# A Strassen decoder trunk: the first quarter of a round and late plain weights without adding DMAs, and a store moved to GpSimd

## The chip, the cores and the metric

The kernel runs on one core of one Trainium2 chip. The metric is the device time of one execution in microseconds. A profiled execution gives the trace: which instruction ran when on TensorE (PE for matmuls, PEld for weight loads), VectorE (DVE), ScalarE (ACT), GpSimd (POOL) and SyncE (SP), when each DMA was issued and landed, and what ended each wait.

## The reference, cut to what matters

Two layers over 512 tokens of width 1024, all in float32. The part that the change touches most is the squared-ReLU MLP of each layer, `h = relu(rms_norm(x) @ w1)`, `x = x + (h * h) @ w2`, with a hidden width of 4096:

```
def sq_relu_mlp(xn, w1, w2):
    h = jax.nn.relu(xn @ w1)
    return (h * h) @ w2

for i in range(2):
    x = x + (diff_attention if i == 0 else retention)(rms_norm(x, norm_mix[i]), ...)
    x = x + sq_relu_mlp(rms_norm(x, norm_mlp[i]), mlp_w1[i], mlp_w2[i])
    gate = jax.nn.sigmoid(rms_norm(x, norm_pe[i]) @ pe_w_gate[i])
    x = x + gate * (p[i] @ pe_w_up[i])
```

The product `p[i] @ pe_w_up[i]` is called the embedding here; layer 1's is the second one.

## The kernel before

**Every float32 product is three matmuls.** A matrix is split into a high part (`hi`, the value rounded to the type float32r) and a low part (`lo`, what is left), and `mm3` (L264 to L266) issues high x high, high x low and low x high. So each weight block that comes from HBM, 128x1024 floats or 512 KB, needs a high and a low tile before TensorE can use it. The tiles are called `wh` and `wl`; there are five buffers of each, and three of the raw block (`raw`).

**How a weight is made (class Weights).** `order` lists all blocks and mixed kinds, 280, in the order of use. `W.next()` hands out the next pair and makes blocks up to four ahead. A plain block is loaded by SP (L91 or L100), ScalarE copies it to `wh`, and then one of two things happens. Where `by_dma` is false, VectorE subtracts: `lo = raw - hi` (L105). Where it is true, ScalarE writes `-raw` to `lo` (L93) and GpSimd issues a DMA that adds `raw` onto `lo` (L94); the raw buffer is read by that DMA until it lands. `by_dma` is set after the first value projection and cleared in the MLP of layer 0.

**The MLP.** Each layer's MLP runs in four chunks of 1024 hidden columns. A chunk first makes eight hidden tiles (`ph`, L768 and after): 24 matmuls of 512 columns each, then ReLU, scale, square, and the split. In the first three chunks the second product goes by Strassen's method (Winograd's form) in two rounds, r = 0 and r = 1, through `mix_round`. A round takes seven products ("kinds") in the order of `MIX`: a11, s1, s2, s4, s3, a12, a22. Each has two halves of 12 matmuls of 256 columns, and its result is added to `x` by VectorE (L729) before the bank is used again. The banks are called `py{layer}{chunk}{round}{bank}`; a11, s2, s3 and a22 use bank b. TensorE takes r = 0 in a slightly mixed order, r = 1 in strict order, a11 first.

**How a kind's weights are made (`mixed`, L108 to L155).** The kinds are quarters of `w2` or sums of them: a11, a21, a22 and a12 are fetched by SP (L118), s1 = a21 + a22 (L129), s2 = s1 - a11 (L132), s4 = a12 - s2 (L136) and s3 = a11 - a21 (L139) on VectorE. ScalarE copies the quarter or sum to `wh` (L146). For a11 and a22 ScalarE also writes `lo = -hi` (L149), and a DMA issued by GpSimd adds the quarter onto it from HBM (L150), a second read of that quarter. For the other five kinds VectorE subtracts (L154). Because of the look-ahead of four, the last quarters of a round and the first kinds of the next are made one behind the other while the round's middle products run.

**What sets the order.** The tile framework orders each engine's instructions by a planner from the program's order and its own estimates; each engine then takes its queue strictly in that order. SP's loads keep the program's order. So an instruction that waits holds back all behind it on its engine.

**The second embedding.** After the retention stage, TensorE makes eight tiles `pu` (L1028), ScalarE copies each out of its bank (L1030), and a DMA issued by ScalarE writes it to DRAM (L1031), from where the last stage reads it. On GpSimd, the last gate products (L1009) come before that point, and the running sum of squares of the next norm (L314) after it.

Of the kernel before, what the change touches and what calls it, by code (L numbers as in the profile page):

```python
# [13 lines left out]
ALU = mybir.AluOpType  # L14
# [50 lines left out]
class Weights:  # L65
# [42 lines left out]
    def mixed(self, kind, w, first):  # L108

        nc, mix = self.nc, self.mix  # L110
        i = len(self.made)

        def source(b):
            return w[first + b // 2 : first + b // 2 + 3 : 2, :, b % 2 * T : b % 2 * T + T].rearrange("j p n -> p j n")

        def fetch(b):
            raw = self.pool.tile([P, 1024], F32, name=f"raw{i}_{b}", tag="raw", bufs=RAW_BUFS)
            self.tc.keep_in_program_order(nc.sync.dma_start(out=raw.rearrange("p (j n) -> p j n", j=2), in_=source(b)))  # L118
            return raw

        def fresh():
            return self.sums.tile([P, 1024], F32, name=f"mix{i}", tag="mix", bufs=2)

        if kind == "a11":
            t = mix["a11"] = fetch(0)
        elif kind == "s1":
            mix["a21"], a22 = fetch(2), fetch(3)
            t = mix["s1"] = fresh()
            nc.vector.tensor_tensor(out=t, in0=mix["a21"], in1=a22, op=ALU.add)  # L129
        elif kind == "s2":  # L130
            t = mix["s2"] = fresh()
            nc.vector.tensor_tensor(out=t, in0=mix["s1"], in1=mix["a11"], op=ALU.subtract)  # L132
        elif kind == "s4":
            mix["a12"] = fetch(1)
            t = fresh()
            nc.vector.tensor_tensor(out=t, in0=mix["a12"], in1=mix["s2"], op=ALU.subtract)  # L136
        elif kind == "s3":
            t = mix["a21"]
            nc.vector.tensor_tensor(out=t, in0=mix["a11"], in1=t, op=ALU.subtract)  # L139
        elif kind == "a12":  # L140
            t = mix["a12"]
        else:
            t = fetch(3)
        hi = self.pool.tile([P, 1024], F32R, name=f"wh{i}", tag="wh", bufs=W_BUFS)
        lo = self.pool.tile([P, 1024], F32R, name=f"wl{i}", tag="wl", bufs=W_BUFS)
        nc.scalar.copy(out=hi, in_=t)  # L146
        if kind in ("a11", "a22"):

            nc.scalar.activation(out=lo, in_=hi.bitcast(F32), func=AF.Copy, scale=-1.0)  # L149
            nc.gpsimd.dma_start(  # L150
                out=lo.rearrange("p (j n) -> p j n", j=2), in_=source(0 if kind == "a11" else 3), accum_op=ALU.add
            )
        else:
            nc.vector.tensor_tensor(out=lo, in0=t, in1=hi.bitcast(F32), op=ALU.subtract)  # L154
        return hi, lo  # L155
# [12 lines left out]
def decoder_trunk(ctx: ExitStack, tc, xT, pT, small, dist, decay, ident,  # L168
                  w_v, w_qk, w_o, w_up0, w1_0, w2_0, w_g0,
                  w_rv, w_rqk, w_rg, w_ro, w_up1, w1_1, w2_1, w_g1, out):  # L170
    nc = tc.nc
# [7 lines left out]
    def ps_mm(name):  # L179
        return psum("mm", 3, name)  # L180
# [13 lines left out]
    def slot(name, dt=F32):  # L194
        return gp.tile([P, T], dt, name=name, tag="slot", bufs=SLOTS)
# [15 lines left out]
    def hidden_order(c):  # L211

        return [f + 4 * a for f in range(4) for a in range(2)] if c < MIXED else list(range(8))
# [48 lines left out]
    def mm3(ps, a, b, start, stop, on=False):  # L262

        nc.tensor.matmul(ps, a[0], b[0], start=start, stop=False, skip_group_check=on)  # L264
        nc.tensor.matmul(ps, a[0], b[1], start=False, stop=False, skip_group_check=on)  # L265
        nc.tensor.matmul(ps, a[1], b[0], start=False, stop=stop, skip_group_check=on)  # L266

    def cols(pair, *ix):
        return tuple(t[(slice(None), *ix)] for t in pair)
# [32 lines left out]
    def make_z(src, gain_col, k, make=slot):  # L302
        zh = make(f"zh{gain_col}_{k}", F32R)
        zl = make(f"zl{gain_col}_{k}", F32R)
        split_into(zh, zl, src, sm[:, gain_col + k : gain_col + k + 1])
        return zh, zl
# [62 lines left out]
    for k in range(KD):  # L369
        t = slot(f"xin{k}")  # L370
# [7 lines left out]
    def up_unit(pu, wu, p, m):  # L378
        for j in range(2):
            o = (m % 4) * 256 + j * P  # L380
            mm3(pu, cols(wu[m // 4], slice(o, o + P)), p[j], j == 0, j == 1)
# [3 lines left out]
    up0, up1 = (dp.tile([KD // 2, P, 2, T], F32, name=f"up{i}") for i in range(2))  # L385


    with tc.tile_pool(name="at", bufs=1) as ap:
# [220 lines left out]
        for what, b in (("qk", 0), ("qk", 1), ("v", 1), ("qk", 2), ("qk", 3)):  # L609
            if what == "qk":  # L610
                qk_at[b] = pos
            for tt in range(NT):
                for k in range(KD):
                    p = tt * KD + k if tt < 2 else 2 * KD + 4 * (k // 2) + 2 * (tt % 2) + k % 2
# [88 lines left out]
    def mlp(z, acc, layer, late_at=2):  # L703
# [43 lines left out]
        with tc.tile_pool(name=f"mlp{layer}", bufs=1) as mp:  # L747
            W.sums = mp
            for c in range(4):
                fs = hidden_order(c)  # L750
                hs, st = [], {}

                def begin(i):
                    if (layer, c, i) == (0, 0, 4):
                        W.by_dma = False
                    return W.next(), ps_mm(f"ph{layer}{c}{i}")

                def unit(s, i, k):
                    mm3(s[1], cols(s[0], slice(k * P, k * P + P)), z[k], k == 0, k == KD - 1)

                def end(s, i):
                    second = i % 2
                    if not second:
                        st["t"] = mp.tile([P, 4, T // 2], F32, name="ht", tag="ht", bufs=2)
                        hs.append([mp.tile([P, 7, T // 2], F32R, name=f"h{part}", tag=f"h{part}", bufs=4) for part in "hl"])
                    t = st["t"]
                    half = t[:, 2 * second : 2 * second + 2, :]
                    nc.vector.scalar_tensor_tensor(  # L768
                        out=half, in0=s[1].rearrange("p (a n) -> p a n", a=2), scalar=0.0,
                        in1=rs.rearrange("p (a n) -> p a n", a=2), op0=ALU.max, op1=ALU.mult,  # L770
                    )
                    nc.scalar.activation(out=half, in_=half, func=AF.Square)
                    h = hs[-1]

                    def put(a, n, src):
                        split_into(h[0][:, a : a + n, :], h[1][:, a : a + n, :], src)

                    if c >= MIXED:
                        put(2 * second, 2, half)
                    elif not second:  # L780
                        put(0, 1, t[:, 0:1, :])
                    else:
                        put(1, 2, half)

                        u = mp.tile([P, 4, T // 2], F32, name="hu", tag="hu", bufs=1)
                        nc.vector.tensor_tensor(out=u[:, 0:2, :], in0=t[:, 1:4:2, :], in1=t[:, 0:2, :], op=ALU.subtract)
                        nc.vector.tensor_tensor(out=u[:, 2, :], in0=t[:, 3, :], in1=u[:, 0, :], op=ALU.subtract)
                        nc.vector.tensor_tensor(out=u[:, 3, :], in0=t[:, 2, :], in1=u[:, 2, :], op=ALU.subtract)
                        put(3, 4, u)

                tiles(8, begin, unit, end, late if c == 0 else None, late_at)
                if c < MIXED:
                    for r in range(2):
                        mix_round(c, r, hs)
                    continue
                for m in range(KD):
                    w = W.next()
                    ps = ps_mm(f"py{layer}{c}{m}")
                    for f in range(8):
                        h = [p[:, 2 * (f % 2) : 2 * (f % 2) + 2, :].rearrange("p a n -> p (a n)") for p in hs[f // 2]]  # L800
                        mm3(ps, cols(w, slice(f * P, f * P + P)), h, f == 0, f == 7)
                    nc.vector.tensor_tensor(out=x[m], in0=x[m], in1=ps, op=ALU.add)
                    if c == 3:
                        if m == 0:
                            nacc = slot(f"acc_p{layer}")
                        zn.append(make_z(x[m], C_PE + 8 * layer, m))
                        squares(nacc, x[m], m)
# [73 lines left out]
    with tc.tile_pool(name="zp", bufs=1) as zp:  # L881
# [9 lines left out]
        with tc.tile_pool(name="ret", bufs=1) as ap:  # L891
# [36 lines left out]
            for h in range(RH):  # L928
# [22 lines left out]
                for n in range(4):  # L951
# [4 lines left out]
                    t = ap.tile([P, T], F32, name="rt", tag="rt", bufs=4)  # L956
# [21 lines left out]
                for jt in range(NT):  # L978
                    n = T - jt * P
# [6 lines left out]
                    t = ap.tile([P, T], F32, name="rt", tag="rt", bufs=4)  # L986
# [39 lines left out]
            for m in range(KD):  # L1026
                pu = (ps_tr if m % 2 == 0 else ps_s)(f"pu1{m}")
                up_unit(pu, wu, p1, m)  # L1028
                t = zslot(f"pus{m}", F32)
                nc.scalar.copy(out=t, in_=pu)  # L1030
                nc.scalar.dma_start(out=up1[m // 2][:, m % 2, :], in_=t)  # L1031
            acc = project(RH - 1, go_before)
            z = zn

# [85 lines left out]
```

## Time and profile before

| | us |
|---|---|
| median of 3 runs | 1477.12 |
| lowest and highest | 1475.58, 1477.51 |
| the profiled execution, whole | 1478.01 |
| its span, first to last instruction | 1476.2 |
| TensorE busy | 1444.1 (98%) |
| VectorE, ScalarE, GpSimd busy | 931.1, 728.0, 184.5 |

The profile's page gives busy times over the whole span; the stages differ much, so stretches and single waits are asked of the trace. A matmul's record lasts longer than the step to the next matmul, since matmuls are pipelined; what counts is the time from start to start.

### The profile page before, as it was taken

To read this page: it belongs to the slowest core of one execution; us is meant where nothing else is said; L and a number is where in the kernel's file an instruction comes from. 1 tells how busy PE (TensorE), PEld (TensorE's weight loads), DVE (VectorE), ACT (ScalarE), POOL (GpSimd) and SP (SyncE) were. 2 spreads that over 40 slices of the span, in tenths; PEclk is the share of its full clock that TensorE was granted. 3 is DMA by queue.
4 is the path that set the end of the run, shared out by engine and by line. 5 is a ranking of instruction groups with operands and counts; after the bars stand their busy time and mean duration, and the time that the engine had idled before them with its cause. 6 is when DMAs were issued, how large, how long until landed. Compare 5 with 4: busy or idle time off the path is not lost.

```text
span 1476.2 us, 19408 instructions
## 1 busy us (share of the span) xinstructions
PE 1444.1 (98%) x7532; PEld 1224.4 (83%) x7532; DVE 931.1 (63%) x1465; ACT 728.0 (49%) x1091; POOL 184.5 (12%) x151
## 2 busy tenths in 40 slices
PE   9999989999999999999999999999999999999998
PEld 7777767889898988888888888888779889898887
DVE  6766777676676764486364555544698576675445
ACT  6777777754444444354442432433565354443432
POOL 4112112100000000211120210301230000000020
PEclk9999999999999999999999999999999999999999
DMA  6644566856355452243223232132334637445332
GB/s 227 143 115 114 129 168 142 216 143 184 104 136 151 113 165 93 63 165 122 79 83 105 65 112 93 58 128 72 129 100 113 173 86 186 114 121 152 98 114 86
DMA packets 65132, 183.14 MB, mean 124 GB/s; under 512 B 6033, under 2 KB 6545, under 8 KB 65041
## 3 DMA queue, kind: packets, MB, share of 16 engines
q1 hardware_dynamic: 51888, 147.31, 30.7%
q0 software_dynamic: 11424, 30.41, 12.0%
q10 hardware_dynamic: 1728, 4.20, 0.8%
q8 instruction: 59, 0.97, 0.3%
q14 instruction: 33, 0.26, 0.1%
HBM read 157.77 MB, written 6.29 MB: 111 GB/s over the span
## 4 chain that ended last, share of the span: by engine, by line
PE 77%; DMA 9%; DVE 5%; ACT 4%; issue 4%; POOL 1%; SPq 0%; DVEq 0%; POOLq 0%; ACTq 0%
PE ph L265 7%; PE ph L264 7%; PE ph L266 7%; DMA raw<-in_w 6%; PE pg L264 2%; PE pg L266 2%; PE pg L265 2%; PE rv L265 2%; PE py L265 2%; PE rqk L265 2%; PE rv L266 2%; PE rqk L266 2%; PE py L266 2%; PE py L264 2%; PE rv L264 2%
## 5 line engine op out<-in xcount | busy, mean ns | idle before, releaser
L101 ACT CAST wh<-raw 128x1024 fp32r<-128x1024 f32 (+1 forms) x163 | 170.2, 1046 | 345.2 <-PE ph L265 85.9
L105 DVE TENSOR_TENSOR wl<-raw,wh 128x1024 fp32r<-128x1024 f32 (+1 forms) x163 | 208.1, 1278 | 62.3 <-ACT wh L101 61.3
L265 PE MATMUL ph<-zl,wh 128*128 128x512 f32 x512 | 199.5, 390 | 0.0
L264 PE MATMUL ph<-zh,wh 128*128 128x512 f32 x512 | 199.3, 389 | 0.0
L266 PE MATMUL ph<-zh,wl 128*128 128x512 f32 x512 | 199.2, 389 | 0.0
L265 PEld LDWEIGHTS ph<-zl,wh 128*128 128x128 f32 x512 | 96.1, 188 | 20.6 <-DVE zl L245 0.8
L266 PEld LDWEIGHTS ph<-zh,wl 128*128 128x128 f32 x512 | 96.1, 188 | 19.9
L264 PEld LDWEIGHTS ph<-zh,wh 128*128 128x128 f32 x512 | 96.1, 188 | 19.8
L768 DVE SCALAR_TENSOR_TENSOR ht<-ph,rsm 128x512 f32<-128x512 f32 x64 | 43.9, 688 | 98.8 <-PE ph L266 98.6
L150 POOL DMA_DIRECT2D wl<-in_w x24 | 29.0, 1281 | 440.5 <-ACT wl L149 375.9
L146 ACT CAST wh<-mix 128x1024 fp32r<-128x1024 f32 x36 | 37.9, 1053 | 86.0 <-PE ph L265 23.3
L146 ACT CAST wh<-raw 128x1024 fp32r<-128x1024 f32 x48 | 49.2, 1049 | 56.3 <-PE ph L265 23.0
L265 PE MATMUL pqk<-wl,zh 128*128 128x512 f32 x128 | 51.1, 399 | 1.2 <-DMA wl<-raw 1.2
L264 PE MATMUL pqk<-wh,zh 128*128 128x512 f32 x128 | 51.6, 403 | 0.0
L264 PE MATMUL pg<-zh,wh 128*128 128x512 f32 (+1 forms) x136 | 51.2, 377 | 0.0
L266 PE MATMUL pg<-zh,wl 128*128 128x512 f32 (+1 forms) x136 | 51.2, 377 | 0.0
L265 PE MATMUL pg<-zl,wh 128*128 128x512 f32 (+1 forms) x136 | 51.2, 376 | 0.0
L266 PE MATMUL pqk<-wh,zl 128*128 128x512 f32 x128 | 51.0, 398 | 0.0
L264 PE MATMUL rg<-zh,wh 128*128 128x512 f32 x128 | 50.2, 392 | 0.0
L265 PE MATMUL rg<-zl,wh 128*128 128x512 f32 x128 | 50.1, 391 | 0.0
L266 PE MATMUL rg<-zh,wl 128*128 128x512 f32 x128 | 50.0, 390 | 0.0
L265 PE MATMUL rv<-wl,zh 128*128 128x512 f32 x128 | 49.8, 389 | 0.0
(1136 smaller groups left out, 4049.2 us busy)
## 6 DMA issues: line engine op xcount, KB each, us to landing
raw<-in_w SPq DMA_DIRECT2D x140, 512.0 KB, 3.8
wl<-raw POOLq DMA_DIRECT2D x34, 512.0 KB, 5.3
wl<-in_w POOLq DMA_DIRECT2D x24, 512.0 KB, 8.1
raw<-in_w_qk SPq DMA_DIRECT2D x16, 512.0 KB, 3.7
raw<-in_w_g SPq DMA_DIRECT2D x16, 512.0 KB, 3.8
raw<-in_w_rv SPq DMA_DIRECT2D x16, 512.0 KB, 3.6
raw<-in_w_rqk SPq DMA_DIRECT2D x16, 512.0 KB, 4.5
raw<-in_w_rg SPq DMA_DIRECT2D x16, 512.0 KB, 3.6
```

The lines of the kernel that those rows point to most:

```text
L101: nc.scalar.copy(out=hi[:, s], in_=raw[:, s])
L105: e.tensor_tensor(out=lo[:, r], in0=raw[:, r], in1=hi[:, r].bitcast(F32), op=ALU.subtract)
L146: nc.scalar.copy(out=hi, in_=t)
L150: nc.gpsimd.dma_start(out=lo.rearrange("p (j n) -> p j n", j=2), in_=source(0 if kind == "a11" else 3), accum_op=ALU.add)
L264: nc.tensor.matmul(ps, a[0], b[0], start=start, stop=False, skip_group_check=on)
L265: nc.tensor.matmul(ps, a[0], b[1], start=False, stop=False, skip_group_check=on)
L266: nc.tensor.matmul(ps, a[1], b[0], start=False, stop=stop, skip_group_check=on)
L768: nc.vector.scalar_tensor_tensor(out=half, in0=s[1].rearrange("p (a n) -> p a n", a=2), scalar=0.0, in1=rs.rearrange("p (a n) -> p a n", a ...
```

## The change

Three edits. In `mixed`, only a22 is still split by ScalarE's negation and an adding DMA; a11 is split by VectorE's subtraction like the other kinds. In the MLP of layer 0, `by_dma` is cleared at the first hidden tile and not at the fifth; as weights are made four ahead, the blocks of hidden tiles 4 to 7 of the first chunk are then split by VectorE, those of 0 to 3 still by adding DMAs. And the eight stores of the second embedding are issued by GpSimd and not by ScalarE.

```
-        if kind in ("a11", "a22"):
+        if kind == "a22":
             nc.scalar.activation(out=lo, in_=hi.bitcast(F32), func=AF.Copy, scale=-1.0)
             nc.gpsimd.dma_start(
-                out=lo.rearrange("p (j n) -> p j n", j=2), in_=source(0 if kind == "a11" else 3), accum_op=ALU.add
+                out=lo.rearrange("p (j n) -> p j n", j=2), in_=source(3), accum_op=ALU.add
             )
         else:
             nc.vector.tensor_tensor(out=lo, in0=t, in1=hi.bitcast(F32), op=ALU.subtract)
...
                 def begin(i):
-                    if (layer, c, i) == (0, 0, 4):
+                    if (layer, c, i) == (0, 0, 0):
                         W.by_dma = False
...
                 nc.scalar.copy(out=t, in_=pu)
-                nc.scalar.dma_start(out=up1[m // 2][:, m % 2, :], in_=t)
+                nc.gpsimd.dma_start(out=up1[m // 2][:, m % 2, :], in_=t)
```

## Rows read from the trace of the kernel before

**Rows 1.** The page's busy times by engine: busy us, share, instructions.

```profile
PE 1444.1 (98%) x7532; PEld 1224.4 (83%) x7532; DVE 931.1 (63%) x1465; ACT 728.0 (49%) x1091; POOL 184.5 (12%) x151
```

**Rows 2.** TensorE's waits, 250 to 1345 us: who for whom, total, times, longest.

```profile
PE py000b L265 <- DVE hl L242: 1.8, 1, 1.8
PE py101b L266 <- DMA wl<-in_w: 1.8, 2, 1.3
PE py021b L266 <- DMA wl<-in_w: 1.4, 1, 1.4
PE py121b L266 <- DMA wl<-in_w: 1.2, 2, 0.8
PE py000b L266 <- DMA wl<-in_w: 1.0, 1, 1.0
PE py011b L266 <- DMA wl<-in_w: 1.0, 1, 1.0
PE py111b L266 <- DMA wl<-in_w: 0.8, 1, 0.8
PE pu L264 <- ACT pus L1030: 0.7, 1, 0.7
PE py001b L264 <- DVE x L729: 0.5, 1, 0.5
PE py001b L266 <- DMA wl<-in_w: 0.5, 1, 0.5
PE py000b L264 <- ACT hh L241: 0.4, 1, 0.4
PE py111b L264 <- DVE x L729: 0.3, 1, 0.3
```

**Rows 3.** The timeline of TensorE: start, us, line, operation, tiles.

```profile
323.12 0.28 PE L266 MATMUL py000b<-hh,wl 128*128 128x256 f32 x1
323.24 0.28 PE L264 MATMUL py000b<-hh,wh 128*128 128x256 f32 x1
```

**Rows 4.** Stretch: length; PE, PEld, DVE, ACT, POOL busy (count); granted clock; DMA.

```profile
324.40:327.80 3.40, 3.40 (x18) 3.40 (x18) 3.40 (x7) 2.21 (x3) 0.00 (x0) 0.51 0.29 77
```

**Rows 5.** The timeline of VectorE, first chunk; brackets: idle before, what ended it.

```profile
311.40 1.23 DVE L129 TENSOR_TENSOR mix<-raw,raw 128x1024 f32<-128x1024 f32 x1 [5.62 <-DMA raw<-in_w]
```

**Rows 6.** The chain that ended last, 300 to 360 us: start, us, what.

```profile
304.92 6.39 DMA raw<-in_w
...
338.16 7.70 DMA raw<-in_w
```

**Rows 7.** The timeline of VectorE at the turn of the second chunk's rounds.

```profile
431.60 1.23 DVE L136 TENSOR_TENSOR mix<-raw,mix 128x1024 f32<-128x1024 f32 x1 [2.81 <-DMA raw<-in_w]
432.74 0.41 DVE L729 TENSOR_TENSOR x<-x,py010b 128x256 f32<-128x256 f32 x1
```

**Rows 8.** The timeline of GpSimd at the same turn.

```profile
421.16 2.42 POOL L150 DMA_DIRECT2D wl<-in_w  x2 [29.00 <-ACT wl L149]
```

**Rows 9.** The timeline of ScalarE at the same turn.

```profile
419.81 2.00 ACT L149 ACTIVATE wl<-wh 128x1024 fp32r<-128x1024 f32 x2
```

**Rows 10.** Line 154, VectorE's difference: count, duration ns min/median/max.

```profile
L154 DVE TENSOR_TENSOR wl<-raw,wh x24: 1212/1216/1225, 324.5 to 1325.0; 128x1024 fp32r<-128x1024 f32 x24
```

**Rows 11.** The second chunk's first round, the same columns as rows 4.

```profile
410.40:431.00 20.60, 20.07 (x168) 19.87 (x166) 14.73 (x24) 9.82 (x11) 2.42 (x2) 1.00 0.64 153
```

**Rows 12.** Line 94, the adding DMA of plain weights: issue ns, landing us.

```profile
L94 POOL DMA_DIRECT2D wl<-raw x34: 850/865/1078, 36.9 to 299.2; - x34
...
DMA to landing us min/median/max: 4.5/5.3/8.3
```

**Rows 13.** Line 150, the adding DMA of quarters: landing us.

```profile
DMA to landing us min/median/max: 5.4/8.1/9.6
```

**Rows 14.** Line 118, the plain load of quarters: landing us.

```profile
DMA to landing us min/median/max: 3.4/3.7/8.3
```

**Rows 15.** The timeline of GpSimd after the retention stage.

```profile
1071.77 3.69 POOL L314 TENSOR_TENSOR acc<-acc,sq 128x512 f32<-128x512 f32 x2 [19.39 <-ACT sq L313]
```

More of the change, by code (lines that the diff above doesn't have):

```diff
@@ L146, in mixed @@
         nc.scalar.copy(out=hi, in_=t)
-        if kind in ("a11", "a22"):
+        if kind == "a22":
             nc.scalar.activation(out=lo, in_=hi.bitcast(F32), func=AF.Copy, scale=-1.0)
             nc.gpsimd.dma_start(
-                out=lo.rearrange("p (j n) -> p j n", j=2), in_=source(0 if kind == "a11" else 3), accum_op=ALU.add
+                out=lo.rearrange("p (j n) -> p j n", j=2), in_=source(3), accum_op=ALU.add
             )
@@ L753, in begin @@
                 def begin(i):
-                    if (layer, c, i) == (0, 0, 4):
+                    if (layer, c, i) == (0, 0, 0):
                         W.by_dma = False
@@ L1030, in decoder_trunk @@
                 nc.scalar.copy(out=t, in_=pu)
-                nc.scalar.dma_start(out=up1[m // 2][:, m % 2, :], in_=t)
+                nc.gpsimd.dma_start(out=up1[m // 2][:, m % 2, :], in_=t)
             acc = project(RH - 1, go_before)
```

## Prediction

> **What bounds the kernel now.** First the page's busy times: TensorE is busy 1444.1 us of a span of 1476.2 [rows 1]. So it is the bound, and an edit gains only what it takes out of TensorE's waits or out of time at a low clock. Next, TensorE's waits in the stretch with both MLPs and the retention stage [rows 2]: the reader is to see that they sit at few places. Most name the adding DMA of a quarter (`wl<-in_w`), six name VectorE's additions to `x`, two the start of the first Strassen round. Third, what one wait costs: in the timeline a 256-column matmul starts every 0.12 us but its record lasts 0.28 [rows 3], so after an idle time the restart costs another 0.16, and I add 0.16 to each wait. Fourth, the clock: after the 1.8 us wait at 323 us, the stretch of 3.40 us from 324.4 has a granted clock of 0.51, the lower level (1.2 GHz), and 18 matmuls, which at 0.12 us are 2.2 [rows 4, 3]; it lost 1.2 us.
>
> **What is there to be won.**
> A. At the start of each second round (bank `py0?1b`, `py1?1b`: six places) TensorE waits for a11's low part: 0.5, 1.0, 1.4, 1.3, 0.8, 0.8 (where a row counts two waits, the longest one is this) = 5.8 us, with six restarts 6.8. Twelve matmuls later it waits for VectorE's addition: 0.5 and five times 0.3 (one of the five stands) = 2.0, with restarts 3.0. Together 9.8 [rows 2].
> B. The first round of all: 1.8 and 0.4 for the hidden split, two restarts, and the 1.2 at the low clock: 3.7 [rows 2, 4].
> C. One wait of 1.0 for a22 at the end of the first round, 1.2 with its restart [rows 2].
> D. In two rows that count two waits, the shorter ones (0.5 and 0.4) are a22 of a second round: 1.2 with restarts [rows 2].
> In all 15.9 us. The wait of 0.7 at `pu` is taken up with the stores.
>
> **Part 1, a11 by VectorE.** Removed are 12 negations on ScalarE of 1.0 us (two took 2.00 [rows 9]) and 12 adding DMAs on GpSimd of 1.2 us (two took 2.42 [rows 8]), with their 512 KB each. Added are 12 differences on VectorE of 1.22 us [rows 10]. Worked out at the turn of the second chunk: both `wh` casts are done when the negations begin, at 419.8 [rows 9], so a11's difference can be done at about 421.0. Before, its adding DMA was issued second of the pair that began at 421.16 [rows 8] and TensorE waited until 431.5. So 10 us of lead take the place of the wait, and this step doesn't need the estimate to be exact.
> What is late next: VectorE stands 2.81 us until 431.60 for the quarter that s4 is made of, and the addition that TensorE's second half of a11 needs is queued behind it, at 432.74 [rows 7]. Were that load not sooner, TensorE would lose at the addition what it gained at a11, since its second half starts when that addition ends, 433.2, whatever went before. So A hangs on the load. Three transfers of 512 KB, two adding and this one, took from 421.16 to about 431.5 [rows 8, 7], 3.4 us each; two of them would be done at 428.0. Without the waits the second half starts at 433.2 - 1.3 - 0.3 = 431.6; the sum takes 1.14 and the addition 0.41, so the load must land by 430.0. It does with 2 us to spare. The bounds are a load alone, 3.4 us, and the longest, 8.3 [rows 14]; I take the middle case and leave 0.15 us at each of six places: A gives 8.9.
> VectorE has the room: in that round it works 14.73 of 20.60 us [rows 11], and 1.22 more is 77%. But TensorE can reuse a bank only after VectorE's addition, and each queue is in order, so a difference at the wrong place delays one by up to 1.22. The bounds for all sixteen differences (four come from part 2) are 0 and 19.5 us. I take 1.2, one of them on the path, since the idle time is five times what is added.
> The six a11 of the first rounds are made while hidden tiles run and had no wait; they give nothing.
> For a22, whose landing took from 5.4 to 9.6 us [rows 13], its companion in the first round's end is gone: of C I take 1.0. In the second round its rivals are the next chunk's plain loads, which stay; but the chain from s4 to it starts up to 3 us sooner. Of D I take half, 0.6.
>
> **Part 2, four plain blocks by VectorE.** Removed are four adding DMAs (0.87 us of GpSimd, 4.5 to 8.3 us to landing [rows 12]) and four ScalarE passes; added are four differences of 1.22. The point is the raw buffer, which such a DMA holds until it lands. The chain at B begins there: a load issued at 304.92 took 6.39 us [rows 6], VectorE stood 5.62 us for it until 311.40 [rows 5], and from then on is late until the hidden split at 323. Freed by a difference 1.2 us long, the buffers come some 4 us sooner for each block, and the load, with two adding DMAs fewer beside it, takes nearer to the 3.7 of its median [rows 14]: the sum can start at 303 to 305, 6 us before. The five new differences before that time (6.1 us) fit into the idle 5.62 and the shorter gaps before it. Support is in layer 1: its first chunk has plain blocks by VectorE already, and no row of `py100b` for a hidden split is among the waits. B goes whole, 3.7, and with the wait the stretch at the lower clock; bounds 0 and 3.7.
>
> **Part 3, the stores.** Eight issues leave ScalarE and come to GpSimd, each behind the copy it stores. GpSimd's queue behind them holds the sums of squares, the first at 1071.77 after 19.39 us of idleness [rows 15]. A plain GpSimd issue took 0.85 to 1.08 us [rows 12]: eight are 6.9 to 8.6, and fit. TensorE's wait at `pu`, 0.7, is for the second copy on ScalarE; it could go (gain 0.9) or, if a store gets in front of a gate product on GpSimd, grow by one issue, 0.9. I take 0. The data are read only in the last stage.
>
> The Trainium skill has a rule against this part: "SBUF — State Buffer", in the section on SBUF's two separate sides, says that GpSimd cannot write the descriptors of its DMAs while certain VectorE instructions hold the port that the two share, and advises to issue from ScalarE or SyncE; it gives 620 ns alone and 3100 beside such an instruction. The row of 34 issues beside a busy VectorE has 850 to 1078 [rows 12], and shows nothing of it. By that factor of five, an estimate from the page's figures, eight stores would take some 35 us, and the time would be about 1479.
>
> **The sum.** 8.9 + 3.7 + 1.0 + 0.6 - 1.2 + 0 = 13.0 us. The profiled execution took 1478.01 us, 1.8 more than its span; less 13.0 it is 1465.0. The median of the runs is 1477.12, 0.9 below that execution, so I forecast 1464.1.
>
> **The rivals.**
> 1. The hidden split stays late (chance 0.13). For it: five more VectorE instructions in a stretch where it was the late engine. Against: it was late because it stood for a load. B is lost: 1464.1 + 3.7 = 1467.8.
> 2. The load for s4 still lands late, and the wait moves from a11 to the addition (0.12). For it: both already wait at the same place, and one adding DMA stays. Against: the 3.4 us per transfer. A is lost: 1464.1 + 8.9 = 1473.0.
> 3. The new differences become the bound (0.06). Place: VectorE's queue in the rounds and in the first chunk. Price: 1.22 each, 19.5 if all are on the path, in place of the 1.2 assumed: 1464.1 + 18.3 = 1482.4. It decides, for slower than before, from 12 of the 16 on the path. The 5.9 us of idle time per round speak against it.
> 4. The stores hold GpSimd (0.03). Place: before the squares at 1071.77. It begins to cost from 19.39 / 8 = 2.4 us a store, and eats the whole gain from (19.39 + 13.0) / 8 = 4.0; at 4.3 us (34.4 in all) it costs 15.0: 1479.1. This is what the skill's rule would do here.
> 5. It doesn't do what it says (0.07): the planner, with other estimates, sets an order in which other waits come up for the ones that go. The time stays about 1476.
>
> **How the numbers follow.** The forecast has 0.59, its own range is 1460 to 1467.5: from all 15.9 won and the wait at `pu` too (1477.1 - 16.8) to one more third of the terms lost. The range for 8 in 10 goes down to 1459.5 and up to 1473.5, which takes in rivals 1 and 2 and leaves out 3, 4 and 5, 0.16. A difference of 0.2% (3.0 us) is about what a measurement of this kernel can tell. Faster by more: the forecast, rival 1 and most of rival 2, 0.83; within: rival 5 and the rest of rival 2, 0.09; slower: rivals 3 and part of 4 and whatever is like them, 0.08.
>
> **What would show it.** For A: no wait of `py?11b` and its kin for `wl<-in_w` at a second round's start, the load for s4 landing in under 6 us, and the `x` waits gone. If the `x` waits have grown to 1 us or more, rival 2 is right. For B: no wait at `py000b` for `hl`, the first sum (L129) near 304 and not 311, and no stretch at the lower clock at 324. For C and D: `wl<-in_w` left as at most two waits under 0.5 us. For part 3: eight GpSimd issues between 1050 and 1070, and the first square still near its place, moved only by what was gained before. The prediction is wrong if the waits go and the span doesn't follow, or if new waits name `wl` of L154 or L105.

## The result, and the profile after

The changed kernel took 1456.37 us (median; 1454.9 to 1457.97) against 1476.35 for the kernel before on the same chip: a ratio of 0.9865 [0.9848, 0.9882], 20.0 us less. Taken a second time in the study it took 1459.49 against 1477.5, 0.9877 [0.9859, 0.9894], 18.0 us less. The forecast was 1464.1 (13.0 us less), so the direction was right and the gain half as large again; the time lies 3 us under the low end of the range. The profiled execution took 1456.06 us, its span 1454.3 (before 1478.01 and 1476.2). One of the ten runs of e3_store_only below took 2026.69 us at a mean granted clock of 0.654 and is left out of its median.

The page of the kernel after, busy times by engine, answers to [rows 1]:

```profile
PE 1434.9 (99%) x7532; PEld 1218.6 (84%) x7532; DVE 948.9 (65%) x1481; ACT 712.8 (49%) x1075; POOL 170.7 (12%) x143
```

VectorE has its 16 differences more and works 17.8 us more, ScalarE has its 16 passes fewer, GpSimd 8 instructions fewer (16 adding DMAs less 8 stores). TensorE's count is unchanged. Its waits of the kernel after, 250 to 1345 us (who for whom, total, times, longest), are this whole answer, beside [rows 2]:

```profile
PE py001b L266 <- DMA wl<-in_w: 0.7, 1, 0.7
PE ro L264 <- ACT oacc L310: 0.3, 1, 0.3
PE rsm1p L323 <- DVE rsm1sl L242: 0.2, 1, 0.2
```

No second round waits for a11, none for an addition to `x`, the first round doesn't wait for the hidden split, `pu` doesn't wait, and of the a22 waits one is left. The wait of 0.3 at `ro`, in the retention stage, is new.

VectorE's timeline in the kernel after, at the turn of the second chunk's rounds ([rows 7]; start, duration, then the instruction, in brackets the idle time before it):

```profile
410.05 1.23 DVE L154 TENSOR_TENSOR wl<-raw,wh 128x1024 fp32r<-128x1024 f32 x1 [0.77 <-ACT wh L146]
...
418.91 1.23 DVE L136 TENSOR_TENSOR mix<-raw,mix 128x1024 f32<-128x1024 f32 x1
420.06 0.41 DVE L729 TENSOR_TENSOR x<-x,py010b 128x256 f32<-128x256 f32 x1
```

The first row is the new a11 difference. The sum for s4 (L136) had stood 2.81 us for its quarter; now no idle time precedes it. That load was issued at 414.10 and landed at 418.82, 4.7 us instead of 7.4. On GpSimd ([rows 8]) one DMA stands where two stood:

```profile
411.28 1.17 POOL L150 DMA_DIRECT2D wl<-in_w  x1 [66.28 <-DVE wl L154]
```

In the first chunk the first sum ([rows 5]: 311.40, after 5.62 us of idleness) starts with the operands already there:

```profile
300.26 1.22 DVE L129 TENSOR_TENSOR mix<-raw,raw 128x1024 f32<-128x1024 f32 x1
```

**Where the time came from.** TensorE's 7532 matmuls come in the same order in these kernels, but for 82 in the first Strassen round (numbers 1526 to 1607, inside B's stretch; in e10 the attention's order differs too), so a matmul can be found in each trace by its number. The table gives, for the stretch around each wait, the time from one numbered matmul to another less the same in the run e8_again (below), which has none of these waits. The letters are those of the prediction; C takes in all a22 of first rounds, and "total" is the whole from the first hidden tile on. "Attention ends" is the start of matmul 1216, one of the attention's last output products. The expectations below call this mark the first hidden tile; that tile itself (`ph`) starts 17.1 us later in every trace, at 275.0 in before.

| trace | attention ends | A | B | C | D | `pu` | other | total |
|---|---|---|---|---|---|---|---|---|
| before | 258.0 | 10.8 | 4.3 | 1.6 | 1.6 | 1.0 | 0.0 | 19.4 |
| before_again | 259.8 | 11.4 | 4.1 | 1.1 | 4.0 | 1.0 | -0.1 | 21.5 |
| after | 254.2 | 0 | 0 | 0 | 1.0 | 0 | 0.2 | 1.2 |
| after_again | 258.7 | 0 | 0 | 0 | 0.8 | 0 | 0.4 | 1.2 |

From the first hidden tile on the change gives 18.2 us in one pair of traces and 20.3 in the other. The rest of the first pair's 21.9 us of span, 3.8, is the attention ahead of it, which scatters with every execution: in the 14 traces of this study this mark lies between 251.3 and 260.5 us.

### The profile page after: what moved, and what is told of

Read it like the earlier page. It is cut to its first block, busy times and chain, and to the rows that moved or that the text cites. A ratio compares the mean times of both kernels' runs of the same rounds, so it can differ in the third digit from the quotient of the medians.

```text
span 1454.3 us, 19337 instructions
## 1 busy us (share of the span) xinstructions
PE 1434.9 (99%) x7532; PEld 1218.6 (84%) x7532; DVE 948.9 (65%) x1481; ACT 712.8 (49%) x1075; POOL 170.7 (12%) x143
## 4 chain that ended last, share of the span: by engine, by line
PE 90%; ACT 3%; DVE 3%; DMA 2%; issue 1%; POOL 0%; SPq 0%; ACTq 0%; POOLq 0%; DVEq 0%
PE ph L265 8%; PE ph L266 8%; PE ph L264 8%; PE rg L264 2%; PE rg L265 2%; PE pg L264 2%; PE pg L266 2%; PE pg L265 2%; PE py L265 2%; PE rqk L265 2%; PE rv L265 2%; PE rv L266 2%; PE rqk L266 2%; PE py L266 2%; PE rv L264 2%; PE rg L266 2%
## 5 line engine op out<-in xcount | busy, mean ns | idle before, releaser
L101 ACT CAST wh<-raw 128x1024 fp32r<-128x1024 f32 (+1 forms) x167 | 174.3, 1046 | 349.4 <-PE ph L265 85.8
L105 DVE TENSOR_TENSOR wl<-raw,wh 128x1024 fp32r<-128x1024 f32 (+1 forms) x167 | 213.1, 1277 | 56.7 <-ACT wh L101 55.5
L264 PE MATMUL ph<-zh,wh 128*128 128x512 f32 x512 | 199.3, 389 | 0.0
L264 PEld LDWEIGHTS ph<-zh,wh 128*128 128x128 f32 x512 | 96.1, 188 | 19.8
L150 POOL DMA_DIRECT2D wl<-in_w x12 | 14.3, 1195 | 462.2 <-DVE wl L154 365.9
L264 PE MATMUL pqk<-wh,zh 128*128 128x512 f32 x128 | 51.6, 403 | 0.0
L264 PE MATMUL pg<-zh,wh 128*128 128x512 f32 (+1 forms) x136 | 51.2, 377 | 0.0
L264 PE MATMUL rg<-zh,wh 128*128 128x512 f32 x128 | 50.2, 392 | 0.0
L264 PE MATMUL rx<-goh,wh 128*128 128x512 f32 x128 | 49.8, 389 | 0.0
```

What stands on the lines that cost most here:

```text
L101: nc.scalar.copy(out=hi[:, s], in_=raw[:, s])
L105: e.tensor_tensor(out=lo[:, r], in0=raw[:, r], in1=hi[:, r].bitcast(F32), op=ALU.subtract)
L150: nc.gpsimd.dma_start(out=lo.rearrange("p (j n) -> p j n", j=2), in_=source(3), accum_op=ALU.add)
```

## The experiments

All ran against the kernel before on the same chip. The theory to test: a wait is lost when the quarter's two adding DMAs and a plain load are in flight together (A, C, D), and when a plain adding DMA holds its raw buffer (B). The rivals: the order of a11 and the sums on VectorE, the change of ScalarE's load, and the differences as a new bound.

**before_again**: the kernel before, unchanged.

> The kernel before, unchanged, for a second trace. The traces of before and after differ by 3.8 us already in the attention, up to the first hidden tile, where both have the same instructions in the same order. Theory 1: that is scatter between executions (a stretch of 3.4 us at the lower clock at 92 us, landings of first loads), so a second trace of before reaches the first hidden tile 1 to 4 us sooner or later than the first did. Theory 2: something of the change reaches back: then this trace agrees with the first one within 0.5 us there, and the single edits show the 3.8 us.

1475.54 us against 1476.66, 0.9987 [0.9971, 1.0002]. Its span differs from that of before by 4.0 us: 1.9 in the attention, 2.4 at D (table), with the same instructions in the same order.

**e1_a11_only**: part 1 alone.

```diff
-        if kind in ("a11", "a22"):
+        if kind == "a22":
```

> Part 1 alone: a11 by VectorE, all else as before. If the terms are independent, it wins the waits for a11 and the additions behind it at six places (11.2 us between the two traces), the a22 waits at the end of first rounds (1.5) and in second rounds (1.1): 13 us faster in all, 1463; the wait at the first round of all, 1.8 us and a stretch at the lower clock, stays. If the gain needs part 2 as well, less than 9 us.

1462.06 us, 0.9905 [0.9881, 0.9929]. Its waits on TensorE, 250 to 1345 us (whole answer):

```profile
PE py021b L266 <- DMA wl<-in_w: 2.2, 1, 2.2
PE py000b L266 <- DMA wl<-in_w: 1.4, 1, 1.4
PE pu L264 <- ACT pus L1030: 0.7, 1, 0.7
PE py000b L264 <- DVE x L729: 0.3, 1, 0.3
PE rsm1p L323 <- DVE rsm1sl L242: 0.2, 1, 0.2
```

A is gone, whole. C is not: the wait of 1.4 at `py000b` is for the first round's a22, which landed after 7.03 us with no a11 DMA beside it, and C costs 1.6 us as in before. That was not expected. Nor was it that B's wait for `hl` is gone: of 4.1 to 4.3 us 0.8 is left. In the kernel before, the first a11's adding DMA was issued just ahead of the load that began at 304.92 [rows 6], as GpSimd's timeline of before has it:

```profile
303.54 1.23 POOL L150 DMA_DIRECT2D wl<-in_w  x1 [3.48 <-ACT wl L149]
```

In e1 it is not there, the same load takes 3.48 us and not 6.39, and VectorE's first sum comes 2.8 us before that of [rows 5]:

```profile
308.64 1.23 DVE L129 TENSOR_TENSOR mix<-raw,raw 128x1024 f32<-128x1024 f32 x1 [1.89 <-DMA raw<-in_w]
```

D is not better here, 3.9 us: the wait of 2.2 is followed by a stretch at the lower clock, granted 0.50 in this trace's window (length, busy times and counts, granted clock, DMA share, GB/s):

```profile
529.50:532.90 3.40, 3.40 (x18) 3.40 (x18) 1.18 (x2) 0.00 (x0) 0.00 (x0) 0.50 0.54 160
```

**e2_plain_only**: part 2 alone.

```diff
-                    if (layer, c, i) == (0, 0, 4):
+                    if (layer, c, i) == (0, 0, 0):
```

> Part 2 alone: the last four plain blocks by VectorE. If freed raw buffers are what counts, the wait for the hidden split at the first round and the stretch at the lower clock go: 4.3 us faster, 1472; all waits of second rounds stay. If the late VectorE was the matter, the wait stays and the time is 1476 to 1478.

1472.04 us, 0.9956 [0.9936, 0.9976]. B is 0, A 9.7, C 0.9, D 3.7, `pu` 1.0: B goes with part 2 and nothing else goes whole.

**e3_store_only**: part 3 alone.

```diff
-                nc.scalar.dma_start(out=up1[m // 2][:, m % 2, :], in_=t)
+                nc.gpsimd.dma_start(out=up1[m // 2][:, m % 2, :], in_=t)
```

> Part 3 alone: the eight stores from GpSimd. If the planner's new order on ScalarE (second copy ahead of the third gate split) comes from this edit, TensorE's wait of 0.7 at pu goes: 0.9 us faster, 1475.5, not to be told from no change by times, but by the trace. If it comes from the earlier start of that stage, the wait stays. If the stores hold up GpSimd, the squares start late and it is slower.

1474.7 us (nine runs), 0.9989 [0.9971, 1.0008]: not to be told from no change by times. By the trace the wait at `pu` is gone and A (11.0), B (3.0), C (1.2) and D (3.7) stay. The cause is an order: in the kernel before, ScalarE's second copy for `pu` stood behind a gate's split (L241) that waited for GpSimd, as ScalarE's timeline of before has it:

```profile
1052.41 0.62 ACT L241 CAST goh<-ro 128x512 fp32r<-128x512 f32 x1 [2.37 <-POOL ro L1009]
1052.94 1.07 ACT L1030 COPY pus<-pu 128x512 f32<-128x512 f32 x2
```

With the stores elsewhere the planner puts both copies ahead of that split (ScalarE's timeline of e3; the kernel after has the same order):

```profile
1043.53 1.07 ACT L1030 COPY pus<-pu 128x512 f32<-128x512 f32 x2
1046.48 0.62 ACT L241 CAST goh<-ro 128x512 fp32r<-128x512 f32 x1 [1.88 <-POOL ro L1009]
```

**e5_spare_dma**: the kernel after, and beside a11's difference the old negation and adding DMA into a spare tile that nothing reads.

```diff
+        if kind == "a11":
+            spare = self.sums.tile([P, 1024], F32R, name=f"spare{i}", tag="spare", bufs=1)
+            nc.scalar.activation(out=spare, in_=hi.bitcast(F32), func=AF.Copy, scale=-1.0)
+            nc.gpsimd.dma_start(
+                out=spare.rearrange("p (j n) -> p j n", j=2), in_=source(0), accum_op=ALU.add
+            )
```

> The kernel after, with a11's negation and adding DMA still run beside VectorE's difference, into a spare tile that nothing reads: the traffic of before, without the dependence. Theory A (the load for s4 decides, and it is late because two adding DMAs share the engines with it): it lands 7 to 8 us after its issue again, VectorE's addition behind it is late, and TensorE waits there, at six places for 1.3 to 2.3 us each, for what the a11 waits gave up: 1465 to 1468. Rival B (the dependence on a11's own low part was all): no such waits, 1456 to 1458.

1472.18 us, 0.9967 [0.9947, 0.9987]. TensorE's waits, 250 to 1345 us (this kernel's lines after 154 are 6 further on: L270 is L264, L735 is L729):

```profile
PE py021b L270 <- DVE x L735: 1.8, 1, 1.8
PE py001b L270 <- DVE x L735: 1.8, 1, 1.8
PE py121b L270 <- DVE x L735: 1.7, 1, 1.7
PE py011b L270 <- DVE x L735: 1.4, 1, 1.4
PE py111b L270 <- DVE x L735: 1.4, 1, 1.4
PE py011b L272 <- DMA wl<-in_w: 0.9, 1, 0.9
...
```

and VectorE's timeline at the turn of the second chunk's rounds:

```profile
424.07 1.23 DVE L136 TENSOR_TENSOR mix<-raw,mix 128x1024 f32<-128x1024 f32 x1 [2.78 <-DMA raw<-in_w]
425.21 0.41 DVE L735 TENSOR_TENSOR x<-x,py010b 128x256 f32<-128x256 f32 x1
```

This is the key run. a11 is ready early and no wait names it, yet A costs 9.4 us of its 10.8, and 1.5 more in a stretch at the lower clock (granted 0.54 from 514.50 to 517.90) behind the wait of 1.8 at `py021b`. With the second adding DMA's traffic back, the quarter for s4 is late again (idle time of 2.78 before the sum, 2.81 in [rows 7]), and the wait stands at the addition behind it. The one of the six places without such a wait, `py101b`, is the one where the load took least, 6.2 us; at the other five it took 7.1 to 8.0. So rival 2's mechanism is real, and what keeps it away in the kernel after is the traffic that went. The time is 4 to 7 us above the 1465 to 1468 expected. The trace of 1470.44 us is longer than e8_again's by 14.1 from the first hidden tile on: A, the 1.5 at the lower clock, D 2.8 and C 0.3. The expectation had left out the low clock and most of D; the median lies 1.7 above this trace.

**e6_a22_by_dve**: the kernel after with the two kinds exchanged: a11 by the adding DMA, a22 by VectorE.

```diff
-        if kind == "a22":
+        if kind == "a11":
...
-                out=lo.rearrange("p (j n) -> p j n", j=2), in_=source(3), accum_op=ALU.add
+                out=lo.rearrange("p (j n) -> p j n", j=2), in_=source(0), accum_op=ALU.add
```

> The kernel after with the two quarters exchanged: a11 by the adding DMA, a22 by VectorE. Theory A (two adding DMAs at one place collide; one alone is in time): a11's part lands some 6 us after its issue, 2 to 3 us before its use; the a22 waits of the second rounds go: 1455 to 1457. Rival B (the first kind of a round is too early for any adding DMA): waits of 0.5 to 1.4 us at six places, 1461 to 1464.

1459.91 us, 0.9868 [0.9833, 0.9902]. The whole answer for TensorE's waits in the same stretch:

```profile
PE rsm1p L323 <- DVE rsm1sl L242: 0.2, 1, 0.2
PE py001b L264 <- DVE x L729: 0.2, 1, 0.2
```

a11 comes by an adding DMA, is needed first, and is in time: its twelve DMAs landed 5.7 to 7.7 us after issue. From the first hidden tile on the trace takes as long as that of the kernel after: A is 1.2 us in short waits for additions, C and D are 0. The median is 3 us above the 1455 to 1457 expected, and this trace's attention is the latest of all (260.5). It was not that a11 went by DMA, but that two went together. The load for s4 shows it at the six turns: it took 7.0 to 8.3 us in before and 6.2 to 8.0 in e5, with two adding DMAs beside it; 3.7 to 5.6 in after and 4.1 to 4.7 in e6, with one; and 3.5 to 3.8 in e8_again, with none. So do VectorE's waits: the row of line 136, which waits for the quarter of s4 (total, times, longest), in before, e5, e6 and after, in this order:

```profile
DVE mix L136 <- DMA raw<-in_w: 18.2, 7, 3.7
```

```profile
DVE mix L136 <- DMA raw<-in_w: 15.9, 6, 3.4
```

```profile
DVE mix L136 <- DMA raw<-in_w: 1.6, 5, 0.4
```

```profile
DVE mix L136 <- DMA raw<-in_w: 0.9, 1, 0.9
```

**e7_reread**: the kernel before, whose last four plain adding DMAs read the weights from HBM again and not from the raw buffer. The DMAs stay, the hold on the buffer goes.

```diff
-            nc.gpsimd.dma_start(out=lo, in_=raw, accum_op=ALU.add)
+            nc.gpsimd.dma_start(out=lo, in_=src if self.again else raw, accum_op=ALU.add)
...
+                    if (layer, c, i) == (0, 0, 0):
+                        W.again = True
```

> The kernel before, but the last four adding DMAs of plain blocks read the block again from HBM and not from the raw buffer, so the buffer is free after ScalarE's two passes; the DMAs, their number and VectorE's work stay. Theory A (the held buffer delays the loads for the first sums): the wait for the hidden split at the first round and the stretch at the lower clock go, 4.3 us faster, 1472. Rival B (the adding DMAs' traffic delays them): as before, 1476, or slower by the 2 MB more.

1473.55 us, 0.9971 [0.9952, 0.999]. B is 0, as in e2, and the first sum starts without idle time (VectorE's timeline; lines one further on):

```profile
301.06 1.22 DVE L130 TENSOR_TENSOR mix<-raw,raw 128x1024 f32<-128x1024 f32 x1
```

So B was the held buffer, not the traffic of those four DMAs. The trace of before shows the hold directly: its last plain adding DMA, issued at 299.20, landed at 304.86, and the load was issued at 304.92. With e1 in mind: this load starts late because of the hold and then takes 6.39 us beside a11's DMA; taking away either was enough for most of B.

**e8_no_quarter_dma and e8_again**: the kernel after with a22 by VectorE too.

```diff
-        if kind == "a22":
+        if kind == "none":
```

> The kernel after with a22 by VectorE as well: no adding DMA in the MLPs. If VectorE has room for twelve more differences of 1.22 us, the one wait left for an adding DMA (0.8 us in the trace) goes: 1455 to 1456. If VectorE is then the late engine in the rounds, waits for its additions (L729) or differences (L154) appear and it is slower than the kernel after, 1458 to 1470.

1455.8 us, 0.9845 [0.9817, 0.9872]. Then the kernel after and this one were run once more on one chip; first what was expected of after_again, then of e8_again:

> The kernel after, unchanged, beside the next one on the same chip. By nine traces so far, what comes before the first hidden tile scatters from 251 to 260 us with the same instructions; the stretch after it should take 1195 to 1197 us again, and the time should be 1455 to 1458.

> The kernel after with a22 by VectorE as well, once more. If the a22 waits of the kernel after are rare (one of 0.8 us in its trace), the two differ by about 1 us and the times can't tell them apart; if a22's waits come and go between executions as they do in the kernel before, where two traces had 1.2 and 3.7 us of them, this one is faster by 1 to 3 us.

After_again took 1459.49 us, 1.5 above its range; from the mark at the attention's end on, its trace takes 1200.0 us and that of after 1200.1, not 1195 to 1197. E8_again took 1457.98, 0.9866 [0.9843, 0.9889]. Its only wait in the stretch is `rsm1p`, 0.2. From the first hidden tile on it is 1.2 us shorter than after by the traces of both pairs; the times (1455.8 and 1457.98 against 1456.37 and 1459.49) can't tell the two apart. By the intervals it is not a better version than after.

**e9_reread_attention and e10_no_adding_dma**: e8, whose attention's adding DMAs read from HBM (e9), or are VectorE's differences (e10, `W.by_dma = True` made `False`).

```diff
-            nc.gpsimd.dma_start(out=lo, in_=raw, accum_op=ALU.add)
+            nc.gpsimd.dma_start(out=lo, in_=src, accum_op=ALU.add)
```

> The kernel without adding DMAs for quarters, and the adding DMAs of plain blocks in the attention read the block again from HBM, so the raw buffers are free sooner there too. If held buffers delay loads in the attention as they did at the first round, the first hidden tile starts 1 to 3 us sooner than the scatter of 251 to 260 us: 1453 to 1455. If the attention waits for VectorE and ScalarE, as its rows say, nothing changes, or the 15 MB more make it slower: 1456 to 1458.

> The kernel without any adding DMA, in the attention too. There VectorE has 30 more differences of 1.22 us (37 us in some 230) and ScalarE 30 passes of 1.05 fewer. If VectorE is the late engine of the attention, it loses 5 to 30 us: 1461 to 1486; if ScalarE is, it gains a few.

1461.22 us, 0.9894 [0.988, 0.9909], and 1458.41, 0.9873 [0.9859, 0.9888]. Neither gains on e8_again's 1457.98 on that chip, and e9 is slower by 3.2. That e10 loses nothing clear of the scatter was a miss. In its first 260 us (PE, PEld, DVE, ACT, POOL busy, granted clock) VectorE works 83% of the time and TensorE does nearly as many matmuls as in the kernel after:

```profile
0.00:260.00 260.00, 245.29 (x1230) 187.46 (x1231) 216.40 (x538) 170.90 (x381) 35.78 (x36) 1.00 0.31 97
```

against the same window of the kernel after,

```profile
0.00:260.00 260.00, 246.41 (x1242) 189.64 (x1243) 188.99 (x513) 195.33 (x410) 58.23 (x63) 1.00 0.59 154
```

Taking away the hold on the raw buffer, worth 4 us at B, gained nothing in the attention. Both runs put something in its place, reads from HBM in e9 and VectorE's work in e10, so that the hold is free there is not shown.

## Why the prediction was right in its main parts and too small

The mechanisms of A and B came as told, and they are most of the gain; that of C did not, though its gain came. The step that failed is "The sum": it has its terms too small. A was put at 8.9 and gave 10.8, the new differences were charged 1.2 and cost nothing, the wait at `pu` was put at 0, between a gain and a loss of 0.9, and gave 1.0. Its 13.0 against the 18.2 of the first pair of traces (terms rounded):

| term | forecast | measured | short by |
|---|---|---|---|
| A | 8.9 | 10.8 | 1.9 |
| B | 3.7 | 4.3 | 0.6 |
| C | 1.0 | 1.6 | 0.6 |
| D | 0.6 | 0.6 | 0 |
| new differences | -1.2 | 0 | 1.2 |
| stores, `pu` | 0 | 1.0 | 1.0 |
| other | 0 | -0.2 | -0.2 |

**A**: the working held. The difference was early, the load landed in 4.7 us where 6 was the limit, and the sum is done before it is needed. Two things were too small. The 0.15 us left at each of six places (0.9) did not stay. And each wait costs more than its idle time and 0.16: over twelve waits 10.8 against 9.8, some 0.1 a wait, which lies in the next matmul (0.07 and 0.10 us more than its usual step at the second chunk's two waits). The traffic estimate of 3.4 us a transfer was good enough: it put the load's landing 6.8 us after a22's issue, and it came after 7.5. E5 and e6 show that the load was the point on which A hung.

**B**: right, in chain and in cause (e2, e7), though e1 shows that part 1 alone would have taken most of it. The first sum came at 300.26; with the 3.8 us by which the attention ended sooner that is 304.1 in the time of before, within the 303 to 305 forecast. The price by rows was 0.6 too small, like A's.

**C and D**: C went whole, but not for the reason given, that its companion is gone. Without the companion e1 still has 1.6 of it; with the companion e5 has 0.3 and e7 0.4. The a22 of first rounds landed after a median of 5.7 us in the six traces with a second adding DMA behind it (e5 and the five named below) and 5.8 in the three without (e1, after, after_again), up to 7.0 in both. So that the change took C away is not shown; it may be luck. For D the traffic counts: the a22 of second rounds landed after a median of 9.1 us in those six traces and 6.4 in the three, and TensorE loses 0.1 us or more to it at three to five places in each of the six and at one in each of the three. But its price is where one trace misled: it cost 1.6, 4.0, 3.7, 3.7 and 2.7 us in the five traces that have both adding DMAs (before, before_again, e3, e2, e7), and the trace that the prediction was made from is the lowest; e1, without a11's DMA, has 3.9. In the second pair of traces D alone gave 3.2. The one wait left in after, 0.7, is over the 0.5 that was to be its limit. A longer wait can bring the lower clock with it, as in e1, so this term is not only scattered but lopsided. The prediction took it from a single row.

**Differences**: 16 more on VectorE cost nothing that shows. In the round of [rows 11] VectorE now works 17.45 of 20.60 us, 85% and not the 77% worked out, since besides the new difference the sum for s4 now comes before the window's end (window of the kernel after, columns as there):

```profile
399.60:420.20 20.60, 20.60 (x172) 20.52 (x171) 17.45 (x27) 9.37 (x10) 1.17 (x1) 1.00 0.49 128
```

At 85% no wait of TensorE in the rounds names it; e8 adds 12 more in the rounds with no loss. Rival 3 was priced from zero to 19.5, and a guess of 1.2 was put in the sum; the idle time of 5.9 us a round was the better reading.

**Stores**: the eight issues came from 1038.4 to 1044.8. All is 13.9 us earlier there (GpSimd's last gate product at 1036.37 against 1050.26), so in the time of before that is 1052.3 to 1058.7, as forecast. The view of line 1031 in the kernel after (durations in ns, minimum, median, maximum):

```profile
L1031 POOL DMA_DIRECT2D up<-pus x8: 540/541/659, 1038.4 to 1044.8; - x8
...
DMA to landing us min/median/max: 3.2/4.5/6.3
```

They cost GpSimd 4.5 us and not 6.9 to 8.6, since the price was taken from issues of adding DMAs [rows 12], and its first square comes at 1056.94, after 11.56 us of idleness. What they changed was ScalarE's order (e3), 1.0 us, which the prediction had named and set to 0. VectorE was busy 3.78 of the 7.0 us from 1038.4 on, and no issue took five times the others. The rule of the Trainium skill weighed before, "SBUF — State Buffer", the section on SBUF's two separate sides, with its 620 against 3100 ns, did not come into play here: all of VectorE's instructions in that stretch are of the kind TENSOR_TENSOR, and no run here puts others beside the stores.

**The rivals**: 1 did not come. Of 5 there is the one new wait of 0.3 at `ro`. 2 did not come, but e5 makes it happen: it was a near thing, decided by one transfer. 3 and 4 are refuted (e8; line 1031).

**The range**: its low end took the whole 16.8 us that one trace's rows offered as the most there could be. The rows of waits understate what waits cost (16.8 worked out, 19.4 lost in that trace), and are one execution's sample of it. Its upper end isn't what it says either: a third of 13.0 is 4.3, which would give 1468.4 and not 1467.5; nothing hung on that.

**Open**: why a22 lands at such different times from one execution to the next, and why the attention's length scatters. In part it is the clock: the five traces with two or three stretches at the lower level in the attention end it at 258.0 to 260.5 us, the six with none at 251.3 to 256.8. Before has one, the kernel after, in its first profile, none. This window is of before:

```profile
92.20:95.60 3.40, 3.40 (x15) 2.81 (x13) 3.21 (x13) 2.42 (x11) 0.00 (x0) 0.50 1.05 173
```

What makes it drop there in one execution and not in another was not tried.

## What to carry to other kernels

Where several transfers are started together, the one that is waited for is not always the one to move: take any one away and look at the second waiter in the same in-order queue, since it is late by the same amount (e5). A buffer that a DMA reads from is held until the DMA lands (at B 5.66 us after its issue); VectorE's difference frees it after 1.22 us, and that can be worth more than the operation costs. When the waits are many and alike, forecast the whole of what they cost, and read scattered ones from more than one trace or widen the range on that side.

## What the runs showed that was not expected

- A wait of 0.3 to 1.4 us in a row of 256-column matmuls costs its idle time and some 0.25 us more, not 0.16 (the twelve waits of A in before: 10.8 us for 7.8 of idle time).
- A plain GpSimd store of 256 KB is issued in 0.54 us (median), less than the 0.865 of an adding DMA from SBUF [rows 12] and the 1.2 of an adding DMA of a quarter. It lands later than from ScalarE's queue: median 4.5 us against 2.5 in before.
- The load beside one adding DMA takes 4.7 us, beside two 7.4, at the same turn of the second chunk. The longest of all loads by L118 is 5.6 after, 8.3 before [rows 14] and 8.0 in e5.
- Of two adding DMAs issued 1 us apart the first does not pay: at that turn a22's landed after 5.6 us in before and 5.8 in after, where it is alone; a11's behind it took 9.2.
- VectorE at 85% of a round's time, in an order made out by the planner, delays TensorE not at all in the kernel after; 30 more differences in the attention cost nothing that the times show.
